# The final norm of a two-layer trunk: the row sums by a matrix of ones

## The chip, the cores and the metric

The kernel runs on one core of one Trainium2 chip. A core has five engines that run side by side and wait for each other by semaphores: TensorE (PE in the profile, with its weight loads as PEld), VectorE (DVE), ScalarE (ACT), GpSimd (POOL) and SyncE (SP), which here issues nearly all DMAs. The metric is the device time of one execution in microseconds (us); the kernel before takes 1105.89 us, the median of three runs that lie between 1105.76 and 1106.03 us. The profile comes from one further execution of the same program.

## The reference

The program is a trunk of two layers (`DEPTH = 2`) over 256 latent tokens and 256 context tokens of 1024 channels. Each layer has a token-mixing part (a normalised and modulated input projection, a convolution branch, neighbourhood attention, gates, an output projection) and a channel-mixing part (a gated MLP with a depthwise convolution of width 3). After the second layer the latent stream `x` goes through one more norm and out:

```python
def rmsnorm(x, g):
    xf = x.astype(jnp.float32)
    y = xf * lax.rsqrt(jnp.mean(xf * xf, axis=-1, keepdims=True) + EPS)
    return (y * g.astype(jnp.float32)).astype(x.dtype)

    x = x + g2 * conv_ffn(h2, w_up[l], ffn_dw[l], ffn_dw_b[l], w_down[l])
    ...
    return rmsnorm(x, final_norm_g)
```

For every token it needs the sum of the squares of its 1024 channels, divided by 1024; from that the reciprocal of the square root; and each channel times this number and times the channel's gain `g`.

## The kernel before

The stream is held transposed: channels lie on the 128 partitions, in `KD = 8` tiles `x[0]` to `x[7]`, and tokens lie along the free dimension, 256 latent ones (`LAT`) and 256 context ones (`CTX`). So the sum over channels runs across partitions, and the kernel makes it with TensorE.

Almost all of the span is one long row of matmuls. Weights come from memory as 512 KB units, are split into a high part (line 167, ScalarE) and a low part (line 168, VectorE), and each product is made of three matmuls (lines 186 to 188). The last such stage is the down projection of layer 1: for each output tile n from 0 to 7 there are 22 steps of three matmuls each; then `residual` adds the result to `x[n]` (line 989, VectorE) and hands `x[n]` to the running sum of squares. There is no planner at the end of the program; each engine runs its instructions in the order in which the code writes them, and what holds an instruction is the semaphore of the engine that makes its operand.

The sum of squares is kept in two parts. `SumSq.add` squares tiles 0 to 6 on ScalarE (line 341) and adds them up in the tile `ss` on VectorE (line 345). The square of the last tile is taken by VectorE (line 337) into a tile `t` of its own and isn't added, so that the two parts are joined on TensorE. Right after `residual` the latent half of `x[n]` is multiplied by the final gain into the half of the tile that held the context (line 1167, ScalarE). Ahead of the last tile the table for the square root is loaded (line 1170).

The tail (lines 1178 to 1200) then does five steps:

1. For each part and each half of 128 tokens, the 128x128 tile of squares is the loaded operand and the column `one` (128x1) is the one that streams. The result is a column `pt[:, t]`, one sum for each token, with tokens on partitions (line 1183, four matmuls of one column).
2. ScalarE takes the root of the 128x2 sums (`std`, shown in the profile as `red`, line 1187).
3. VectorE takes the reciprocal of the 128x2 roots (`rs`, line 1188).
4. TensorE spreads it: each column of `rs`, broadcast to 128 columns, is transposed against the identity, so that every partition holds the 256 numbers along the free dimension (`po`, line 1191, two instructions).
5. VectorE multiplies the eight tiles by `po` (line 1196), and SyncE stores the result: two DMAs of half a buffer, and then three whole ones (lines 1198 and 1200).

The scratch tiles `t` are a ring of five buffers of 128x512 (`tmp()`); `red` and `rs` are of small pools of their own. The accumulation banks `pt` and `po` are one each.

Of the kernel before, what the change touches and what calls it, by code (L numbers as in the profile page):

```python
# [11 lines left out]
AF = mybir.ActivationFunctionType  # L12
ALU = mybir.AluOpType
AX = mybir.AxisListType

P = 128
D = 1024
# [15 lines left out]
LAT, CTX = slice(0, S), slice(S, 2 * S)  # L33
# [20 lines left out]
def trunk(ctx: ExitStack, tc: tile.TileContext, xt, cvec, crow, wall, wada, params, bias_t, rope_t, out):  # L54
    nc = tc.nc
    pe, act, dve, pool, sp = nc.tensor, nc.scalar, nc.vector, nc.gpsimd, nc.sync
# [11 lines left out]
    def nm(s):  # L68
        uid[0] += 1
        return f"{s}_{uid[0]}"  # L70
# [3 lines left out]
    def psum(tag="main"):  # L74
        return psp.tile([P, 512], F32, tag=tag, bufs=BANKS[tag], name=nm(tag))

    def tmp(w=512):
        return tp.tile([P, w], F32, tag="t", bufs=5, name=nm("t"))

    def small(shape, tag, bufs=2):  # L80
        return tp.tile(shape, F32, tag=tag, bufs=bufs, name=nm(tag))

    def sl(w, i):
        return w[:, i * P : (i + 1) * P]
# [14 lines left out]
    def whole(g):  # L99

        while True:
            try:
                next(g)
            except StopIteration as e:
                return e.value
# [8 lines left out]
    start = ExitStack()  # L114
# [5 lines left out]
    ident = cp.tile([P, P], F32, name="ident")  # L120
    make_identity(nc, ident)
    one = cp.tile([P, 1], F32, name="one")
# [4 lines left out]
    eps = cp.tile([P, 1], F32, name="eps")  # L127
# [193 lines left out]
    x = [t[:, i] for t in x2 for i in range(2)]  # L321
# [26 lines left out]
    def sum_squares(n, T, apart=False):  # L348

        at = tp.tile([P, 512], F32, tag="ss", name=nm("ss"))  # L350
        return [SumSq(T, at[:, i * T : (i + 1) * T], apart) for i in range(n)]
# [266 lines left out]
    for l in range(DEPTH):  # L618
# [5 lines left out]
        with ExitStack() if last else start as e1a:  # L624
# [75 lines left out]
            with ExitStack() as e1b:  # L700
# [27 lines left out]
                if l == 0:  # L728
# [39 lines left out]
                    pb = tp.tile([P, 512], F32, tag="ss", name="rstd0")  # L768
# [44 lines left out]
                else:  # L813
                    sp.dma_start(rope, rope_t)
                    pg0 = [psum("sc") for _ in range(2)]
                    for uu in range(2):
                        wg = wunit(l, U_GLU0 + uu)
                        for i in range(2):
                            for kk in range(4):
                                k = 4 * uu + kk  # L820
# [88 lines left out]
            with ExitStack() as e1c:  # L909
# [69 lines left out]
                for n, pc in branch(U_CO, sh_, sl_):  # L979
                    t = tmp()[:, :T]  # L980
# [27 lines left out]
                sss = sum_squares(NS, S)  # L1008
# [15 lines left out]
                for s in range(NS if held else 0):  # L1024
                    for n, w in zip(range(NB, KD), held):
                        c = slice(s * S, (s + 1) * S)
# [12 lines left out]
        with ExitStack() as e2:  # L1039
# [45 lines left out]
            if last:  # L1085
# [3 lines left out]
                for k in range(KD):  # L1089
# [4 lines left out]
                    if k == 6:  # L1094
                        pb = whole(sums)
# [48 lines left out]
            sss = sum_squares(NS, S, last)  # L1144
# [7 lines left out]
            for streams, ns in [((0, 1), range(NB)), *(((s,), range(NB, KD)) for s in range(NS))]:  # L1152
                wu = None
                c = slice(streams[0] * S, (streams[-1] + 1) * S)
                for n in ns:
                    ps = psum()
                    for k in range(KF):
                        t = n * KF + k
# [17 lines left out]


            if last:
                std, rs = small([P, 2], "red"), small([P, 2], "rs")
                pt = psum("pt")  # L1180
                for i, p in enumerate(sss[0].parts):
                    for t in range(2):
                        pe.matmul(
                            pt[:, t : t + 1], sl(p, t), one, start=i == 0 and t == 0, stop=i == len(sss[0].parts) - 1,
                            skip_group_check=True,
                        )
                act.activation(std, pt[:, 0:2], AF.Sqrt, bias=eps, scale=1.0 / D)
                dve.reciprocal(rs, std)
                pb = psum("po")
                for t in range(2):  # L1190
                    pe.transpose(sl(pb, t), rs[:, t : t + 1].to_broadcast([P, P]), ident)
                for k in range(0, KD, 2):
                    y = tmp()
                    for i in range(2):
                        c = slice(i * S, (i + 1) * S)
                        dve.tensor_tensor(y[:, c], x[k + i][:, CTX], pb[:, LAT], ALU.mult)
                        if k == 0:
                            sp.dma_start(out[0][:, c], y[:, c])
                    if k:
                        sp.dma_start(out[k // 2], y)  # L1200
# [124 lines left out]
```

## Time and profile before

| what | us |
| --- | --- |
| median of three runs | 1105.89 |
| the profiled execution, by the same clock as the runs | 1106.48 |
| its span in the profile | 1104.7 |
| start of the last matmul of the down projection | 1095.54 |
| start of the first multiply of the tail (line 1196) | 1098.55 |
| end of the last multiply | 1101.29 |

All times in the trace are counted from the start of the span. The profile lists each group of instructions with its engine, source line, operation and operands, written as result<-inputs. A row of the trace in order of time gives the start, the duration, the engine and the line, and in brackets how long the engine had been idle before it and which instruction released it. The granted clock of TensorE is 0.998 over the span. A matmul on full f32 data shows as two matmul records with a weight load each; transposes show as one.

### The profile page before, as it was taken

To read this page: it belongs to the slowest core of one execution; us is meant where nothing else is said; L and a number is where in the kernel's file an instruction comes from. 1 tells how busy PE (TensorE), PEld (TensorE's weight loads), DVE (VectorE), ACT (ScalarE), POOL (GpSimd) and SP (SyncE) were. 2 spreads that over 40 slices of the span, in tenths; PEclk is the share of its full clock that TensorE was granted. 3 is DMA by queue.
4 is the path that set the end of the run, shared out by engine and by line. 5 is a ranking of instruction groups with operands and counts; after the bars stand their busy time and mean duration, and the time that the engine had idled before them with its cause. 6 is when DMAs were issued, how large, how long until landed. Compare 5 with 4: busy or idle time off the path is not lost.

```text
span 1104.7 us, 18020 instructions
## 1 busy us (share of the span) xinstructions
PE 1092.2 (99%) x6886; PEld 949.0 (86%) x6886; DVE 895.9 (81%) x1630; ACT 567.6 (51%) x943; POOL 43.8 (4%) x59
## 2 busy tenths in 40 slices
PE   8999999999999999999999999999999999999997
PEld 6777777788889888888888888989889999999997
DVE  5568898889988788888888556789799888988773
ACT  4458767445334544443433223444676667666642
POOL 1111110011000000000000000000000000000000
PEclk9999999999999999999999999999999999999999
DMA  9888673988843445544567665556644484666781
GB/s 364 287 225 223 145 169 103 288 245 214 260 133 115 131 141 167 151 154 153 172 191 230 208 187 181 181 187 212 190 132 141 151 279 150 204 191 177 230 261 56
DMA packets 59510, 209.26 MB, mean 189 GB/s; under 512 B 7200, under 2 KB 7456, under 8 KB 59424
## 3 DMA queue, kind: packets, MB, share of 16 engines
q1 hardware_dynamic: 54384, 190.77, 53.6%
q0 software_dynamic: 4752, 17.30, 8.2%
q8 instruction: 54, 0.88, 0.3%
q14 instruction: 32, 0.26, 0.1%
q10 hardware_dynamic: 288, 0.04, 0.0%
HBM read 187.63 MB, written 1.05 MB: 171 GB/s over the span
## 4 chain that ended last, share of the span: by engine, by line
PE 87%; DVE 4%; ACT 3%; DMA 3%; SPq 1%; issue 1%; DVEq 0%; ACTq 0%
PE main L186 26%; PE main L188 25%; PE main L187 25%; PE main L723 4%; DMA raw<-in_wall 2%; SPq L715 1%; PE sc L186 1%; PE sc L187 1%; PE sc L188 1%; PE po L219 1%; PE po L564 1%; ACT whi L167 1%; DVE cb L659 1%; DVE wlo L168 1%; PE sc L481 1%
## 5 line engine op out<-in xcount | busy, mean ns | idle before, releaser
L186 PE MATMUL main<-h,whi 128*128 128x256 f32 (+1 forms) x1328 | 447.3, 337 | 0.0
L188 PE MATMUL main<-h,wlo 128*128 128x256 f32 (+1 forms) x1328 | 443.3, 335 | 1.1 <-DVE wlo L168 1.1
L187 PE MATMUL main<-h,whi 128*128 128x256 f32 (+1 forms) x1328 | 442.6, 334 | 0.1
L167 ACT CAST whi<-raw 128x1024 fp32r<-128x1024 f32 (+1 forms) x211 | 217.7, 1036 | 240.9 <-DMA raw<-in_wall 116.1
L168 DVE TENSOR_TENSOR wlo<-raw,whi 128x1024 fp32r<-128x1024 f32 (+1 forms) x211 | 253.2, 1207 | 90.2 <-ACT whi L167 86.7
L186 PEld LDWEIGHTS main<-h,whi 128*128 128x128 f32 x1328 | 249.6, 188 | 30.4 <-issue 2.2
L188 PEld LDWEIGHTS main<-h,wlo 128*128 128x128 f32 x1328 | 249.4, 188 | 29.8 <-DVE wlo L168 1.5
L187 PEld LDWEIGHTS main<-h,whi 128*128 128x128 f32 x1328 | 249.9, 188 | 28.5 <-DVE h L391 0.5
L659 DVE SCALAR_TENSOR_TENSOR cb<-u,par,cb 128x512 f32<-128x512 f32 (+1 forms) x240 | 144.3, 617 | 2.8
L187 PE MATMUL main<-fl,whi 128*128 128x256 f32 (+1 forms) x386 | 122.9, 319 | 0.0
L186 PE MATMUL main<-fh,whi 128*128 128x256 f32 (+1 forms) x386 | 122.9, 319 | 0.0
L188 PE MATMUL main<-fh,wlo 128*128 128x256 f32 (+1 forms) x386 | 122.9, 318 | 0.0
L293 DVE CUSTOM_DVE_ANT_0 t<-raw,sb,par 128x1024 bf16<-128x1024 f32 x72 | 91.6, 1280 | 0.6 <-DMA raw<-in_wada 0.3
L187 PEld LDWEIGHTS main<-fl,whi 128*128 128x128 f32 x386 | 72.7, 188 | 5.6
L186 PEld LDWEIGHTS main<-fh,whi 128*128 128x128 f32 x386 | 72.7, 188 | 5.6
L188 PEld LDWEIGHTS main<-fh,wlo 128*128 128x128 f32 x386 | 72.7, 188 | 5.5
L1052 ACT ACTIVATE t<-main,par 128x512 f32<-128x512 f32 (+1 forms) x82 | 50.8, 668 | 38.4 <-PE main L188 38.4
L293 DVE CUSTOM_DVE_ANT_0 t<-own,sb,par 128x1024 bf16<-128x1024 f32 x48 | 60.4, 1281 | 2.9 <-DMA own<-in_wada 2.9
L205 ACT CAST whi<-raw 128x1024 fp32r<-128x1024 f32 x33 | 34.6, 1050 | 49.5 <-PE main L187 42.5
L1053 DVE SCALAR_TENSOR_TENSOR t<-main,par,t 128x510 f32<-128x510 f32 (+1 forms) x82 | 47.6, 616 | 9.8 <-ACT t L1052 9.4
L1056 DVE SCALAR_TENSOR_TENSOR t<-main,par,t 128x510 f32<-128x510 f32 (+1 forms) x82 | 46.8, 611 | 0.0
L390 ACT ACTIVATE h<-t,mod 128x256 fp32r<-128x256 f32 x56 | 25.2, 502 | 34.9 <-DVE t L389 34.7
(216 smaller groups left out, 1259.0 us busy)
## 6 DMA issues: line engine op xcount, KB each, us to landing
raw<-in_wall SPq DMA_DIRECT2D x240, 512.0 KB, 4.4
raw<-in_wada SPq DMA_DIRECT2D x64, 512.0 KB, 4.5
wlo<-raw POOLq DMA_DIRECT2D x33, 512.0 KB, 5.6
own<-in_wada SPq DMA_DIRECT2D x24, 512.0 KB, 5.6
bias<-in_bias_t SPq DMA_DIRECT2D x8, 520.0 KB, 5.1
row<-in_wada SPq DMA_DIRECT2D x8, 512.0 KB, 4.8
sb<-in_crow SPq DMA_DIRECT2D x5, 512.0 KB, 4.9
x<-in_xt SPq DMA_DIRECT2D x4, 512.0 KB, 5.1
```

The source lines that it names most:

```text
L167: act.copy(hi[:, c], r[:, c])
L168: dve.tensor_tensor(lo[:, c], r[:, c], hi[:, c].bitcast(F32), ALU.subtract)
L186: pe.matmul(ps, w[0], xh, start=start, stop=False)
L187: pe.matmul(ps, w[0], xl, start=False, stop=False)
L188: pe.matmul(ps, w[1], xh, start=False, stop=stop)
L205: act.copy(hi, r)
L293: dve.tensor_tensor_reduce(tmp().bitcast(BF16), r, v, 1.0, pr(l, BADA + n, 1), ALU.mult, ALU.add, mods[l][:, n, s : s + 1])
L659: dve.scalar_tensor_tensor(cb[j], src, w, cb[j], ALU.mult, ALU.add)
L723: mm = pe.matmul(pv[t], h1[n == 1][k][:, c], w[n == 2][:, b], start=k + n == 0, stop=k == KD - 1 and n == 2)
L1052: act.activation(c, pv_, AF.Identity, bias=pr(l, FDB + t, 1), scale=w[1])
L1053: dve.scalar_tensor_tensor(c[:, :, 1:], pv_[:, :, : S - 1], w[0], c[:, :, 1:], ALU.mult, ALU.add)
L1056: dve.scalar_tensor_tensor(c[:, :, : S - 1], pv_[:, :, 1:], w[2], c[:, :, : S - 1], ALU.mult, ALU.add)
```

## The change

The sums are now made the other way round. The column `one`, broadcast to a 128x128 matrix of ones, is the loaded operand, and the 128x256 tile of squares streams past it. So each of the 128 output partitions holds the same row of 256 sums, and they need not be spread any more. The root is taken on the whole 128x256 block from the bank `po` into a tile of the `t` ring, the reciprocal is taken in that tile in place, and the multiplies read it there instead of reading `po`. The four matmuls of one column and the two transposes go; two matmuls of 256 columns come. The root and the reciprocal stay one instruction each but are 128 times as wide. The multiplies, the stores and everything before the tail are unchanged.

```diff
             if last:
-                std, rs = small([P, 2], "red"), small([P, 2], "rs")
-                pt = psum("pt")
+                pb, std = psum("po"), tmp()[:, LAT]
                 for i, p in enumerate(sss[0].parts):
-                    for t in range(2):
-                        pe.matmul(
-                            pt[:, t : t + 1], sl(p, t), one, start=i == 0 and t == 0, stop=i == len(sss[0].parts) - 1,
-                            skip_group_check=True,
-                        )
-                act.activation(std, pt[:, 0:2], AF.Sqrt, bias=eps, scale=1.0 / D)
-                dve.reciprocal(rs, std)
-                pb = psum("po")
-                for t in range(2):
-                    pe.transpose(sl(pb, t), rs[:, t : t + 1].to_broadcast([P, P]), ident)
+                    pe.matmul(pb[:, LAT], one.to_broadcast([P, P]), p[:, LAT], start=i == 0, stop=i == len(sss[0].parts) - 1)
+                act.activation(std, pb[:, LAT], AF.Sqrt, bias=eps, scale=1.0 / D)
+                dve.reciprocal(std, std)
                 for k in range(0, KD, 2):
                     y = tmp()
                     for i in range(2):
                         c = slice(i * S, (i + 1) * S)
-                        dve.tensor_tensor(y[:, c], x[k + i][:, CTX], pb[:, LAT], ALU.mult)
+                        dve.tensor_tensor(y[:, c], x[k + i][:, CTX], std, ALU.mult)
```

On TensorE this is the end of the program; the first two rows are the last two products of the down projection, and in each row the result stands left of the arrow, the streamed operand first behind it and the loaded one second.

```order
 L187 MATMUL main_11534<-fl_21_10871,whi_11584 128x256
 L188 MATMUL main_11534<-fh_21_10870,wlo_11585 128x256
-L1183 MATMUL pt_11619<-one,ss_10874 128x1 x2
-L1183 MATMUL pt_11619<-one,t_11614 128x1 x2
-L1191 MATMUL po_11626<-ident,rs_11618 128x128 x2
-L1320 UNCONDITIONAL_BRANCH
+L1181 MATMUL po_11617<-ss_10874,one 128x256
+L1181 MATMUL po_11617<-t_11614,one 128x256
```

Six instructions become two, and TensorE has nothing left to do behind the reciprocal.

On VectorE this is the end of the program from the last residual on; `t_11614` is the square of the last tile, `po_11626` the spread reciprocal of before, and `t_11618` the tile that now holds root and reciprocal.

```order
 L989 SCALAR_TENSOR_TENSOR x_110<-main_11534,mod_106,x_110 128x256
 L337 TENSOR_TENSOR t_11614<-x_110 128x256
-L1188 RECIPROCAL rs_11618<-red_11617 128x2
-L1196 TENSOR_TENSOR t_11629<-x_107,po_11626 128x256 x2
-L1196 TENSOR_TENSOR t_11634<-x_108,po_11626 128x256 x2
-L1196 TENSOR_TENSOR t_11638<-x_109,po_11626 128x256 x2
-L1196 TENSOR_TENSOR t_11642<-x_110,po_11626 128x256 x2
-L1320 UNCONDITIONAL_BRANCH
+L1183 RECIPROCAL t_11618<-t_11618 128x256
+L1188 TENSOR_TENSOR t_11623<-x_107,t_11618 128x256 x2
+L1188 TENSOR_TENSOR t_11628<-x_108,t_11618 128x256 x2
+L1188 TENSOR_TENSOR t_11632<-x_109,t_11618 128x256 x2
```

No instruction changes its place in the row; the reciprocal grows from 2 columns to 256, and the first multiply now waits for VectorE itself and no longer for TensorE.

## The prediction

> **What bounds the kernel now.** I read the page's busy shares and its chain first, then the trace in order of time over the last ten microseconds, and then single lines for the durations. The page says that TensorE carries the span:
>
> ```profile
> span 1104.7 us, 18020 instructions
> PE 1092.2 (99%) x6886; PEld 949.0 (86%) x6886; DVE 895.9 (81%) x1630; ACT 567.6 (51%) x943; POOL 43.8 (4%) x59
> ...
> PE 87%; DVE 4%; ACT 3%; DMA 3%; SPq 1%; issue 1%; DVEq 0%; ACTq 0%
> ```
>
> The edit touches nothing before the last matmul of the down projection, and only what follows that matmul is a chain in which one engine hands to the next. This is the trace in order of time from that matmul to the end (start, duration, engine, line, result<-inputs, idle time before and who ended it):
>
> ```profile
> 1095.54 0.28 PE L188 MATMUL main<-fh,wlo 128*128 128x256 f32 x1
> 1095.55 0.53 PEld L1183 LDWEIGHTS pt<-one,ss 128*128 128x128 f32 x4
> 1095.66 0.50 PE L1183 MATMUL pt<-one,ss 128*128 128x1 f32 x4
> 1095.87 0.48 DVE L989 SCALAR_TENSOR_TENSOR x<-main,mod,x 128x256 f32<-128x256 f32 x1 [6.44 <-PE main L188]
> 1096.38 0.43 DVE L337 TENSOR_TENSOR t<-x 128x256 f32<-128x256 f32 x1
> 1096.38 0.51 ACT L1167 ACTIVATE x<-x,par 128x256 f32<-128x256 f32 x1 [5.51 <-DVE x L989]
> 1096.86 0.52 PEld L1183 LDWEIGHTS pt<-one,t 128*128 128x128 f32 x4 [0.78 <-DVE t L337]
> 1096.86 0.61 PE L1183 MATMUL pt<-one,t 128*128 128x1 f32 x4 [0.70 <-DVE t L337]
> 1097.57 0.26 ACT L1187 ACTIVATE red<-pt,eps 128x2 f32<-128x2 f32 x1 [0.68 <-PE pt L1183]
> 1097.86 0.17 DVE L1188 RECIPROCAL rs<-red 128x2 f32<-128x2 f32 x1 [1.05 <-ACT red L1187]
> 1098.08 0.19 PEld L1191 LDWEIGHTS po<-ident,rs 128*128 128x128 f32 x2 [0.70 <-DVE rs L1188]
> 1098.08 0.43 PE L1191 MATMUL po<-ident,rs 128*128 128x128 f32 x2 [0.61 <-DVE rs L1188]
> 1098.55 2.74 DVE L1196 TENSOR_TENSOR t<-x,po 128x256 f32<-128x256 f32 x8 [0.52 <-PE po L1191]
> 1099.00 0.82 SPq L1198 DMA_DIRECT2D out<-t  x2
> 1099.99 1.66 SPq L1200 DMA_DIRECT2D out<-t  x3
> ```
>
> Each idle time in brackets names the step just before it, so from 1095.87 on there is no slack: square, sums, root, reciprocal, spread, multiply, store. The edit works on the stretch from the end of the square (1096.38 + 0.43 = 1096.81) to the first multiply (1098.55), which is 1.74 us. All stores come behind it, so what this stretch gains or loses moves the end by as much. It is 0.16% of the span; 0.2% (2.2 us) is about what a measurement of this kernel can tell from no change.
>
> **The change part by part.** The sum is made against the profiled execution, 1106.48 us with 1104.7 us of span, and its difference is then put on the median of the runs, 1105.89 us; that execution stood 0.59 us above the median.
>
> *Matmuls on `ss`.* They are covered: `ss` was ready before, its four short records start at 1095.66 and TensorE then idles 0.70 us. Two records of 256 columns start at the same place and end well before 1096.86. If that cover went, they would cost what follows for `t`.
>
> *Matmuls on `t`.* The rows for full f32 matmuls of 128 and 256 streamed columns, the load of a 128x128 operand, and the other rows that this part needs (minimum/median/maximum in ns):
>
> ```profile
> L591 PE MATMUL pt<-one,t x32: 273/273/377, 6.1 to 10.7; 128*128 128x128 f32 x32
> L219 PE MATMUL po<-raw,sil x128: 379/379/403, 10.9 to 48.4; 128*32 128x256 f32 x128
> L359 PEld LDWEIGHTS pt<-one,ss x32: 186/192/192, 234.3 to 912.9; 128*128 128x128 f32 x32
> L521 ACT ACTIVATE pp<-sc,mx x8: 463/470/474, 113.4 to 179.1; 128x256 f32<-128x256 f32 x8
> L677 ACT ACTIVATE t<-main 128x256 f32<-128x256 f32 x3 | 1.1, 380 | 1.7 <-PE main L188 1.7
> L1052 ACT ACTIVATE t<-main,par 128x256 f32<-128x256 f32 x40 | 20.3, 557 | 0.9 <-PE main L188 0.9
> L982 DVE TENSOR_TENSOR t<-t,g 128x256 f32<-128x256 f32 x8 | 3.2, 420 | 0.0
> L1196 DVE TENSOR_TENSOR t<-x,po 128x256 f32<-128x256 f32 x8 | 2.7, 415 | 0.5 <-PE po L1191 0.5
> L317 DVE SCALAR_TENSOR_TENSOR gain<-mod,par 128x2 f32<-128x2 f32 x23 | 3.2, 157 | 0.2
> ```
>
> 128 more columns take 379 - 273 = 106 ns, so 256 columns stream in 0.21 us. There are two records, since f32 shows two per instruction here: 0.21 for the first and 0.38 for the second, 0.59 us against the 0.61 us of the short ones, -0.02. The loaded ones don't depend on `t`, so I take the load as hidden; where it still starts only when `t` is there, it adds 0.19. If the streaming took two more passes, it would add 0.42. Both ends go into the range.
>
> *Root.* From 128x2 to 128x256, out of an accumulation bank. The nearest row is L521, a function with a pointer bias and 256 columns from such a bank: 0.47 against 0.26 us, +0.21. The ends are L677 without the pointer (0.38, +0.12) and L1052 with two pointers (0.56, +0.30). The root's table was loaded at line 1170 in both kernels, so nothing is added for it.
>
> *Reciprocal.* This is the term that decides, and no row shows it wide. These are all the reciprocals of the trace by line, and below them two single ones that both started after a wait:
>
> ```profile
> L507 DVE RECIPROCAL ri<-sm x32: 155/158/166, 86.9 to 833.5; 128x1 f32<-128x1 f32 x32
> L523 DVE RECIPROCAL ri<-sm x8: 156/162/168, 114.4 to 183.6; 128x2 f32<-128x2 f32 x8
> L1188 DVE RECIPROCAL rs<-red x1: 165/165/165, 1097.9 to 1097.9; 128x2 f32<-128x2 f32 x1
> ...
> L507 DVE RECIPROCAL ri<-sm x1: 164/164/164, 86.9 to 86.9; 128x1 f32<-128x1 f32 x1
> L523 DVE RECIPROCAL ri<-sm x1: 166/166/166, 114.4 to 114.4; 128x2 f32<-128x2 f32 x1
> ```
>
> One column or two cost about 0.16 us, nearly all of it fixed. What a further column costs can only be bounded. An ordinary elementwise instruction grows by (420 - 157) / 254 = 1.04 ns a column (L317 to L982); that is the low end, 0.165 + 254 x 0.00104 = 0.43 us. The high end is the largest reciprocal of two columns against the smallest of one, 168 - 155 = 13 ns, or 3.47 us. The pair after a wait differs by 2 ns and speaks for the low end. The nearest row is L1188 itself, the very instruction that is widened, 165 ns against a median of 158 for one column: 7 ns a column. I take this, because a division isn't a product and nothing in the trace shows one running at a column per product's time: 0.165 + 254 x 0.007 = 1.94 us against 0.165, +1.78. The bounds are +0.26 and +3.30.
>
> [...]
>
> *Spread.* The two transposes go. From the end of the reciprocal (1097.86 + 0.17 = 1098.03) to the first multiply at 1098.55 it was 0.52 us. In its place comes VectorE's wait for its own result; the nearest such handover is L989 to L337, 1096.38 - (1095.87 + 0.48) = 0.03 us. -0.49.
>
> *Multiplies.* They read two tiles and no bank: 420 against 415 ns in the rows. Eight of them ran in 2.74 us, one each 0.33 us, so they overlap, and the 5 ns count at most once each, 0 to 0.04; I take 0. `t_11618` is a fifth tile in the ring of five, and so the last multiplies take over the buffer of `t_11614`; its reader, the matmul on `t`, is over by then, since root and reciprocal lie between, so that wait is empty.
>
> *Stores.* Unchanged in number and order; they start later by the sum.
>
> Sum: -0.02 + 0.21 + 1.78 - 0.49 = +1.48 us. With g ns for each further column of the reciprocal it is -0.30 + 0.254 g: zero at g = 1.2, and +2.2 us at g = 9.9. On the profiled execution this is 1107.96, and on the median 1105.89 + 1.48 = 1107.4 us.
>
> **The rivals.**
>
> *The reciprocal streams like any elementwise instruction.* For it speaks the pair after a wait (164 and 166 ns); against it only that it is a division. With g = 1.04 the sum is -0.04, 1105.85 us. If the root is also as short as L677, it is -0.13, 1105.8. This is the case that ends on the other side: the two transposes and their handovers are gone and nothing has taken their place. It decides if g is under 1.2 ns.
>
> *The reciprocal takes longer still.* At g = 13, the widest reading of the rows, the sum is +3.0, 1108.9 us, slower by 0.27%; it decides from g = 9.9. That high end sets a waited-for record against one that hadn't waited, which speaks against it.
>
> *The ones must be loaded behind `t`, or streaming takes longer.* +0.19 or +0.42 on top of whichever reciprocal holds: 1107.6 to 1107.8 with mine. For the first speaks that the load for `t` waited in the trace (0.78 us, ended by L337); there, however, the loaded operand was `t` itself.
>
> *The stores bound the tail, so that the chain before them matters less.* The tail in two stretches, before and after the last multiply's end:
>
> ```profile
> 1098.55:1101.29 2.74, 0.00 (x0) 0.00 (x0) 2.74 (x8) 0.00 (x0) 0.00 (x0) 0.91 0.45 158
> 1101.29:1104.70 3.41, 0.00 (x0) 0.00 (x0) 0.00 (x0) 0.00 (x0) 0.00 (x0) 0.50 0.49 181
> ```
>
> The DMA share is 0.45 and 0.49 and all of it lies behind the first multiply, so no store can hide a later reciprocal. I give this no chance of its own.
>
> **How the numbers follow.** A reciprocal of some 4 to 9.9 ns a column: 0.55, with times from 1106.6 to 1108.1. One that streams, g up to 2 or so: 0.33, with 1105.6 to 1106.1. Over 9.9 ns, or a slow division with the ones loaded late on top: 0.10. Something else: 0.02. The likeliest is the first, at 1107.4. The range reaches to the streaming case below and a little past 0.2% above, 1105.6 to 1108.2; the likeliest case's own range is 1106.6 to 1108.1. Faster by over 0.2% needs 2.2 us from a stretch of 1.74 us, 0.01; slower by over 0.2% is the third case and part of the first's upper end, 0.14; the rest, 0.85, is within 0.2%.
>
> **What would show it.** In the profile after: a reciprocal of 128x256 of about 1.9 us (0.4 if it streams); a root of 0.47 us; two matmul records on `t` of 0.59 us together; a gap of 0.03 us between reciprocal and multiply; eight multiplies in 2.7 us; and the last 3.4 us as they were. The prediction is wrong in its main step if the reciprocal stays under 1 us, and wrong in its frame if the span before 1095.5 has moved.

## The result and the profile after

The changed kernel takes 1107.97 us, the median of 22 runs, against 1105.99 us for the kernel before in the same sessions: 1.98 us more. The ratio is 1.0015 with a 95% interval of 1.0009 to 1.0021, which is 1.0 to 2.3 us more; 1.0015 itself is 1.7 us, so the two medians lie further apart than the ratio says. The means of the same runs are 1107.79 and 1106.22 us, 1.57 us apart. The growth is under the 0.2% that the prediction took for the least that can be told from no change, but the whole interval lies above 1, so the two kernels are told apart.

The trace of the changed kernel in order of time, from the last matmul of the down projection to the end:

```profile
1095.20 0.28 PE L188 MATMUL main<-fh,wlo 128*128 128x256 f32 x1
1095.20 0.30 PEld L1181 LDWEIGHTS po<-ss,one 128*128 128x128 f32 x2
1095.32 0.59 PE L1181 MATMUL po<-ss,one 128*128 128x256 f32 x2
1095.52 0.48 DVE L989 SCALAR_TENSOR_TENSOR x<-main,mod,x 128x256 f32<-128x256 f32 x1 [6.43 <-PE main L188]
1096.04 0.42 DVE L337 TENSOR_TENSOR t<-x 128x256 f32<-128x256 f32 x1
...
1096.51 0.30 PEld L1181 LDWEIGHTS po<-t,one 128*128 128x128 f32 x2 [1.01 <-DVE t L337]
1096.52 0.70 PE L1181 MATMUL po<-t,one 128*128 128x256 f32 x2 [0.60 <-DVE t L337]
1097.25 0.47 ACT L1182 ACTIVATE t<-po,eps 128x256 f32<-128x256 f32 x1 [0.71 <-PE po L1181]
1097.76 1.75 DVE L1183 RECIPROCAL t<-t 128x256 f32<-128x256 f32 x1 [1.30 <-ACT t L1182]
1099.55 2.77 DVE L1188 TENSOR_TENSOR t<-x,t 128x256 f32<-128x256 f32 x8
1100.00 0.82 SPq L1190 DMA_DIRECT2D out<-t  x2
1101.00 1.67 SPq L1192 DMA_DIRECT2D out<-t  x3
```

The stretch from the end of the square (1096.04 + 0.42 = 1096.46) to the first multiply (1099.55) was 1.74 us and is 3.09 us now. More than half of it is one instruction, the reciprocal of 128x256. The stretches of multiplying and storing are what they were, here with the busy time of each engine in turn (PE, PEld, DVE, ACT, POOL), the granted clock, the DMA share and GB/s:

```profile
1096.46:1099.55 3.09, 0.70 (x2) 0.30 (x2) 1.76 (x3) 0.56 (x2) 0.00 (x0) 1.00 0.00 0
1099.55:1102.32 2.77, 0.00 (x0) 0.00 (x0) 2.77 (x8) 0.00 (x0) 0.00 (x0) 0.70 0.45 158
1102.32:1105.70 3.38, 0.00 (x0) 0.00 (x0) 0.00 (x0) 0.00 (x0) 0.00 (x0) 0.50 0.48 181
```

The multiplies took 2.74 us before and take 2.77 now; the last stretch was 3.41 us and is 3.38. So the trace shows the growth of 3.09 - 1.74 = 1.35 us in one place. The two profiled executions differ by less than that, 1107.50 - 1106.48 = 1.02 us, since the last matmul of the down projection, which the edit doesn't touch, started 0.34 us earlier in the second one.

### The profile page after: what moved, and what is told of

Its sections match the earlier page's. It is cut to its first block, busy times and chain, and to the rows that moved or that the text cites. A ratio compares the mean times of both kernels' runs of the same rounds, so it can differ in the third digit from the quotient of the medians.

```text
span 1105.7 us, 18006 instructions
## 1 busy us (share of the span) xinstructions
PE 1091.8 (99%) x6880; PEld 948.0 (86%) x6880; DVE 897.5 (81%) x1630; ACT 568.0 (51%) x943; POOL 43.5 (4%) x59
## 4 chain that ended last, share of the span: by engine, by line
PE 96%; DVE 2%; ACT 1%; issue 0%; DMA 0%; DVEq 0%; ACTq 0%
PE main L186 28%; PE main L188 28%; PE main L187 28%; PE main L723 4%; PE sc L186 1%; PE sc L188 1%; PE sc L187 1%; PE po L564 1%; PE sc L481 1%; PE po L219 1%; PE pt L481 1%; PE sc L547 0%; ACT t L1052 0%; DMA x<-in_xt 0%; ACT whi L167 0%
```

## The experiments

**Without the reciprocal.** The multiplies use the root itself, so that the output is left with the wrong factor and the division is missing.

```diff
                 act.activation(std, pb[:, LAT], AF.Sqrt, bias=eps, scale=1.0 / D)
-                dve.reciprocal(std, std)
```

> The changed kernel without its reciprocal: the multiplies use the root itself, so the output is the stream times its root mean square; the division is left out. If the wide reciprocal is all that the change loses, the stretch from the end of the square to the first multiply falls from 3.09 us to 3.09 - 1.75 - 0.04 = 1.30 us, which is 0.44 us under the 1.74 us of the kernel before; the time is 0.4 us under before, 1105.5, ratio 0.9996. Rival: part of the 2.0 us between the medians lies outside this stretch (the stretch itself grew by 1.35 only); then this kernel is still slower than before by some 0.2 to 0.6 us, ratio above 1.0002, though its stretch is short.

Its trace in order of time:

```profile
1096.54 0.42 DVE L337 TENSOR_TENSOR t<-x 128x256 f32<-128x256 f32 x1
...
1097.02 0.70 PE L1181 MATMUL po<-t,one 128*128 128x256 f32 x2 [0.60 <-DVE t L337]
1097.75 0.47 ACT L1182 ACTIVATE t<-po,eps 128x256 f32<-128x256 f32 x1 [0.70 <-PE po L1181]
1098.26 2.77 DVE L1187 TENSOR_TENSOR t<-x,t 128x256 f32<-128x256 f32 x8 [1.30 <-ACT t L1182]
```

The stretch runs from 1096.96 to 1098.26, 1.30 us as expected and 0.44 us under the kernel before. The time can't confirm it: 1105.72 against 1105.90 us, ratio 0.9999 with an interval of 0.9990 to 1.0008, which holds both the 0.9996 of the theory and the rival's values, 1.0002 and a little above. What the trace says is plain, though. Of the 0.44 us, 0.17 are the narrow reciprocal of the kernel before and 0.03 the step from the root to it, which have nothing in their place here. The rest, 0.44 - 0.17 - 0.03 = 0.24 us, is what sums, root and the missing spread gain together, and the wide reciprocal turns that into a loss.

**Three reciprocals in a row.**

```diff
                 dve.reciprocal(std, std)
+                dve.reciprocal(std, std)
+                dve.reciprocal(std, std)
```

> The changed kernel with the reciprocal taken three times in a row in place, so that the result is the reciprocal again. If it lies on the path with its whole length, two more of them add 2 x (1.75 + 0.04) = 3.58 us to the stretch, 6.67 us in all, and the time is 1105.99 + 1.35 + 3.58 = 1110.9 us, ratio 1.0045 to before. Rival: the long reciprocal in the trace is partly a start-up of the first wide one, or is partly hidden; then the second and third are shorter than 1.7 us or the time rises by less than 3 us.

```profile
1096.12 0.43 DVE L337 TENSOR_TENSOR t<-x 128x256 f32<-128x256 f32 x1
...
1097.85 1.75 DVE L1183 RECIPROCAL t<-t 128x256 f32<-128x256 f32 x1 [1.30 <-ACT t L1182]
1099.63 1.75 DVE L1184 RECIPROCAL t<-t 128x256 f32<-128x256 f32 x1
1101.42 1.75 DVE L1185 RECIPROCAL t<-t 128x256 f32<-128x256 f32 x1
1103.21 2.77 DVE L1190 TENSOR_TENSOR t<-x,t 128x256 f32<-128x256 f32 x8
```

All three are equally long, 1.79 us from start to start. The stretch is 1103.21 - 1096.55 = 6.66 us against the 6.67 expected, and the time 1111.16 against 1105.90 us: 5.26 us more, ratio 1.0048 (1.0035 to 1.0060, so 3.9 to 6.7 us), where 4.9 were expected. A reciprocal here lies on the path with its whole length, and there is no start-up in the first.

**A ladder of widths.** Behind the last multiply, on a scratch tile, a reciprocal and then a square of each width:

```diff
+                lad = tmp()
+                dve.memset(lad, 1.5)
+                for n in (1, 2, 4, 8, 16, 32, 64, 128, 256, 512):
+                    dve.reciprocal(lad[:, :n], lad[:, :n])
+                dve.memset(lad, 1.0)
+                for n in (1, 2, 4, 8, 16, 32, 64, 128, 256, 512):
+                    dve.tensor_tensor(lad[:, :n], lad[:, :n], lad[:, :n], ALU.mult)
```

> The changed kernel with work added behind the last multiply: reciprocals in place on 1, 2, 4, ... 512 columns of a scratch tile, then squares on the same widths. Its own time says nothing; each duration is read. If the reciprocal costs 6.25 ns for each column from the second on (1.752 us at 256 columns less 0.165 at 2, over 254), the widths 1, 4, 16, 64, 256, 512 take about 0.16, 0.18, 0.26, 0.55, 1.75, 3.35 us and the product 0.16, 0.16, 0.17, 0.22, 0.42, 0.69. Rival one: a fixed part hides the first columns, so that up to 8 or 16 columns both operations take the same and the slope starts only there, which would be why one and two columns told so little. Rival two: the long one in the tail is long for another reason (its place behind ScalarE), and 256 columns take well under 1.7 us here.

Groups by line and shape, costliest first, with some rows in between left out; the number before the last bar is the duration in ns. `L1196` is the ladder's reciprocal, `L1199` its product, and `L1183` the reciprocal of the tail in the same run:

```profile
L1196 DVE RECIPROCAL t<-t 128x512 f32<-128x512 f32 x1 | 3.4, 3353 | 0.0
L1196 DVE RECIPROCAL t<-t 128x256 f32<-128x256 f32 x1 | 1.8, 1754 | 0.0
L1183 DVE RECIPROCAL t<-t 128x256 f32<-128x256 f32 x1 | 1.8, 1753 | 1.3 <-ACT t L1182 1.3
L1199 DVE TENSOR_TENSOR t<-t 128x512 f32<-128x512 f32 x1 | 0.7, 692 | 0.0
L1196 DVE RECIPROCAL t<-t 128x64 f32<-128x64 f32 x1 | 0.6, 553 | 0.0
L1199 DVE TENSOR_TENSOR t<-t 128x256 f32<-128x256 f32 x1 | 0.4, 426 | 0.0
L1196 DVE RECIPROCAL t<-t 128x16 f32<-128x16 f32 x1 | 0.3, 253 | 0.0
L1196 DVE RECIPROCAL t<-t 128x8 f32<-128x8 f32 x1 | 0.2, 203 | 0.0
L1196 DVE RECIPROCAL t<-t 128x4 f32<-128x4 f32 x1 | 0.2, 178 | 0.0
L1196 DVE RECIPROCAL t<-t 128x2 f32<-128x2 f32 x1 | 0.2, 166 | 0.0
L1196 DVE RECIPROCAL t<-t 128x1 f32<-128x1 f32 x1 | 0.2, 164 | 0.0
L1199 DVE TENSOR_TENSOR t<-t 128x1 f32<-128x1 f32 x1 | 0.2, 159 | 0.0
```

From 2 columns to 512 the reciprocal follows one line: (3353 - 166) / 510 = 6.25 ns a column, with a fixed part of 153 to 154 ns. (The widths not shown, 32 and 128, took 353 and 953 ns and lie on it.) The product grows by (692 - 159) / 511 = 1.04 ns. Rival one falls in the form that it had: nothing hides eight columns, since 4 already take 12 ns more than 2. But one column lies 4 ns above the line (164 where it gives 160), so that the step from one column to two shows 2 ns and not 6. Rival two falls too: 1754 ns here, 1753 in the tail of the same run.

**Spread the root, then divide.** The kernel before, with the reciprocal moved behind the spread. The transposes now spread the root, and the reciprocal takes 256 columns out of the bank instead of 2 out of a tile. It writes a scratch tile, and the multiplies read that tile.

```diff
-                std, rs = small([P, 2], "red"), small([P, 2], "rs")
+                std = small([P, 2], "red")
...
                 act.activation(std, pt[:, 0:2], AF.Sqrt, bias=eps, scale=1.0 / D)
-                dve.reciprocal(rs, std)
-                pb = psum("po")
+                po, pb = psum("po"), tmp()[:, LAT]
                 for t in range(2):
-                    pe.transpose(sl(pb, t), rs[:, t : t + 1].to_broadcast([P, P]), ident)
+                    pe.transpose(sl(po, t), std[:, t : t + 1].to_broadcast([P, P]), ident)
+                dve.reciprocal(pb, po[:, LAT])
...
-                        dve.tensor_tensor(y[:, c], x[k + i][:, CTX], pb[:, LAT], ALU.mult)
+                        dve.tensor_tensor(y[:, c], x[k + i][:, CTX], pb, ALU.mult)
```

> The kernel before with one part changed: sums by columns and root on 128x2 as before, the two transposes spread the root, and the reciprocal is taken after them on 128x256, out of the bank into a tile. No matrix of ones. If the width of the reciprocal alone makes the loss, the stretch is 1.74 - 0.165 - 0.05 + 1.75 + 0.04 = 3.3 us, longer even than with the change (3.09), and the time is 1.6 us above before, 1107.6, ratio 1.0014. Rival: the matrix of ones (its load and its two passes of 256 columns) or the wide root carries a good part; then the stretch stays under 2.7 us and the time within 1 us of before.

```profile
1095.64 0.43 DVE L337 TENSOR_TENSOR t<-x 128x256 f32<-128x256 f32 x1
...
1096.12 0.60 PE L1183 MATMUL pt<-one,t 128*128 128x1 f32 x4 [0.70 <-DVE t L337]
1096.82 0.26 ACT L1187 ACTIVATE red<-pt,eps 128x2 f32<-128x2 f32 x1 [0.68 <-PE pt L1183]
...
1097.13 0.43 PE L1190 MATMUL po<-ident,red 128*128 128x128 f32 x2 [0.41 <-ACT red L1187]
1097.60 1.76 DVE L1191 RECIPROCAL t<-po 128x256 f32<-128x256 f32 x1 [1.54 <-PE po L1190]
1099.40 2.77 DVE L1196 TENSOR_TENSOR t<-x,t 128x256 f32<-128x256 f32 x8
```

The stretch is 1099.40 - 1096.07 = 3.33 us, with 3.3 expected, and the time 1107.66 against 1105.90 us, ratio 1.0016 (1.0007 to 1.0024). The other steps kept their lengths: the sums on `t` took 0.60 us (0.61 before), the root 0.26 (0.26), and from the root to the reciprocal it was 1097.60 - (1096.82 + 0.26) = 0.52 us, as before from the reciprocal to the multiply. Without any matrix of ones the kernel is as slow as with it. So the width of the reciprocal makes the loss by itself. With the matrix of ones the stretch is 3.33 - 3.09 = 0.24 us shorter, the same 0.24 as in the first experiment: that part of the change gains a little.

## Why the prediction was right, and where not

The forecast was 1107.4 us, slower by 1.48 us on the sum, and inside 0.2%. The median came out 1.98 us up, the stretch in the trace 1.35. The mechanism was right: the wide reciprocal costs more than the spread that it saves. The sum missed the stretch by 1.48 - 1.35 = 0.13 us, mainly by the size of the reciprocal, as the steps show:

- *Frame.* It held. Nothing before the tail was changed, no slack lay in the chain, and the stores moved with it: 2.77 and 3.38 us against 2.74 and 3.41. The last matmul of the down projection started 0.34 us earlier than in the profile before. That is no effect of the edit as far as the traces tell: over the profiles of the two kernels and the four experiments, which share all code before the tail, this start lies anywhere between 1094.80 and 1095.70.
- *Matmuls on `t`.* Forecast -0.02. From the start of the first of them to the start of the root it was 1097.57 - 1096.86 = 0.71 us and is 1097.25 - 1096.52 = 0.73, so +0.02. The profile splits this into 0.70 - 0.61 = +0.09 for the matmuls and -0.07 for the time from the last of them to the root (0.10 and 0.03 us). The ends of matmuls are modelled in it, though, and the sum of the two is surer than the split. The third rival was partly right: the load of the ones for `t`, which needs nothing of `t`, started at 1096.51 after 1.01 us of idle time that ended with L337. The two records of the covered `ss` pair took 0.59 us together, just the sum of the working; those on `t` took 0.11 more. In the kernel before it was 0.50 on `ss` and 0.61 on `t`, the same 0.11, so the working set records that follow others directly against a group that starts after a wait. On `ss` the first load began 0.11 or 0.12 us ahead of the first matmul, on `t` it began with it. That the late load makes these 0.11 us is likely, but no run separates it from other costs of starting after a wait. There were two records, not four.
- *Root.* Forecast +0.21, measured 474 - 263 = +0.21. L521 was the right row. These are the single lines of the changed kernel:

```profile
L1181 PE MATMUL po<-ss,one x2: 377/378/378, 1095.3 to 1095.5; 128*128 128x256 f32 x2
L1181 PE MATMUL po<-t,one x2: 379/431/483, 1096.5 to 1096.8; 128*128 128x256 f32 x2
L1182 ACT ACTIVATE t<-po,eps x1: 474/474/474, 1097.3 to 1097.3; 128x256 f32<-128x256 f32 x1
L1183 DVE RECIPROCAL t<-t x1: 1752/1752/1752, 1097.8 to 1097.8; 128x256 f32<-128x256 f32 x1
```

- *Reciprocal.* Forecast +1.78, measured 1752 - 165 = +1.59. The case was right: the division costs 6.25 ns a column and a product 1.04. That 7 ns a column came near 6.25 was luck, because the reason given for 7 doesn't stand. It set L1188, which had started after a wait, against the median of one-column rows that mostly had not. The pair of rows after a wait, with its 2 ns, was the cleaner comparison, and it pointed the wrong way, as the ladder's own step from 1 to 2 columns does (164 to 166). One column lies above the line on which all the others lie. The rival that streams was built on that pair, and it falls by 1.3 us. The rival at 13 ns falls as well.
- *Spread.* Forecast -0.49. The gap between reciprocal and first multiply is 1099.55 - (1097.76 + 1.75) = 0.04 us where it was 0.52: -0.48.
- *Multiplies.* Forecast 0, measured 2.77 - 2.74 = +0.03, behind the stretch. They ran without a wait, as was said, though the square, the root and the four outputs make six tiles for the ring of five, and the root's is the second of them.

The measured terms of the stretch give 0.02 + 0.21 + 1.59 - 0.48 = +1.34, against the 1.35 read. The forecast had the reciprocal 0.19 us too dear and the matmuls 0.04 too cheap.

The medians lie 1.98 us apart, 0.63 more than the stretch. Most of that is the choice of the median: the means of the same runs differ by 1.57 us, 0.22 more than the stretch. By their means the experiments lie above their stretches as well, by 0.23, 0.21 and 0.13 us (without the reciprocal, with three, with the root spread), though these three were set against the same runs of the kernel before. Each stretch lies within the interval of its measured time, so these 0.2 us need not be anything; but no run here shows that they are nothing.

## What to carry to other kernels

An instruction whose time grows with its columns should see each number once. Here 256 reciprocals laid out as 128x2 cost 0.17 us, and the same 256 numbers copied to every partition cost 1.75, so spread the result, and not what it is made from. The exception is a cheap operation: all terms but the reciprocal gained 0.25 us here (0.02 + 0.21 - 0.48), so by an estimate the two forms come out even at 0.25 / 254, about 1 ns a column, which is a product's cost; no run tried one. And a rate isn't to be read from one and two columns: a few widths far apart, added to a run behind the kernel's own work, settle it.

## What the runs showed that was not expected

- The reciprocal on VectorE costs 6.25 ns a column at 128 partitions in f32, six times a product's 1.04, out of a tile or out of an accumulation bank (1.75 and 1.76 us for 256 columns), and 3.35 us for 512.
- The constant operand of this matmul was not loaded ahead of the wait for the streamed one: TensorE was idle 0.60 us before the matmul on `t`, and the load of the ones still came at 1096.51, with the matmul.
